# Moving a register load, the first rows' copies, four idle products and the order of the last products in a hybrid layer with a routed mixture of experts

## The chip, the cores and the metric

One core of one Trainium2 chip runs one launch. The metric is device microseconds of that launch; the time given is a median of runs without a profile. A profile is one more execution, taken by the hardware profiler. Times inside it count from the start of its span. Engines: PE multiplies (PEld loads its weights), DVE, ACT and POOL work on tiles in on-chip memory, SP issues most transfers.

## The reference

A pre-norm layer on 512 tokens of width 1024. The mixer and the router come first; what matters here is the mixture of experts behind them (one of 4 groups for each token, and two of its 8 experts):

```python
g_idx = jnp.argmax(g_logits, axis=-1)
top_p, top_i = lax.top_k(e_probs, TOP_K)
combine = (g_onehot[:, :, None] * (g_weight[:, None] * e_w)[:, None, :]).astype(x.dtype)
for g in range(N_GROUPS):
    h = jax.nn.silu(jnp.einsum('nd,edf->nef', xt, w_gate[g])) * jnp.einsum('nd,edf->nef', xt, w_up[g])
    out = out + jnp.einsum('nef,efd->nd', h * combine[:, g, :, None], w_down[g])
```

Then the result is added to the residual `h`, and a last RMSNorm gives the output. Each of 32 experts has three matrices of 2 MB in float32, 201 MB in all, and all of them are read.

## The kernel before, in words

The kernel is one function, `layer_kernel`, whose order on each engine is as written (a manual schedule): attention and spatial gating with the input projection, the output projection with the router inside it, then the experts in 16 pairs, then a tail.

**Router's end.** `rows_mm` (L853) sums where each expert's rows lie into `sps`; 8 products at L934 sum the tokens of each expert into `pos_ps`. `rows` (L858, L860) makes `gi`, the indices by which `gather` (L939) fetches the rows of later pairs from the stored `xn_d`. The rows of pair 0 don't come by gather: `first_rows` (L758) has them in PSUM tiles `px0` (`pf` in the profile), and `with_gain` (L973 on ACT, four copies; L975 on DVE, one) copies them into `xs0`.

**Counts.** From `pos_ps` DVE makes `cnt`, `cov`, `cop`, `tot` and `okt`. An expert has 64 slots (`SLOTS`); rows over them go to an overflow path (`over_1`, `over_2`, `gate_up_over`, `down_over`) under conditionals, `if_over`, one for each pair (L1215, L1174), whose counts are loaded into registers when they are reached (L1156). If the overflow is over 32 rows, a general path behind the tail does the rest: its count is `n_over`, loaded at L1153 on PE, ACT, DVE and SP; the conditional that reads it stands behind the tail.

**Pairs.** `gu(a)` and `gu(b)` are the gate and up products of the two experts (L1011, 16 products of 512 columns each), `act` the gate (L1017 to L1023), `down` (L1041) the down products into `y_0` and `y_1` for the two halves of the width, `results` (L1061 on ACT, L1062 on DVE) splits them into `yh` and `yl`, and `combine` of the pair before adds them to the tokens' rows with one-hot products (`oh`, L1051; `add_rows`, L1069) and DVE's `into_h` (L1075). From p = 1 on the overflow's conditionals stand behind `gu(b)` and behind `down`.

**Weights.** `load_next` issues transfers from SP in a fixed order, each 128 x 2048 floats, into 19 slots; each waits for PE to have read the slot's last content, and for an earlier transfer on its own semaphore. The last slot is in pool `mo`, which takes the memory of the router's pool `rw`.

**Tail.** For the last pair: `down` for `y_0`, `results`, `places` (`oh`), `down` for `y_1`, `results`; then `unit` (L1069, L1270, L1075) adds pair and overflow into `h` for four chunks and half 0 (`cl_0`), `squares` (L1260) sums for the norm, `gained` (L1275) multiplies by the gain, then half 1 (`cl_1`), `scale_3` (L1264, L1265), `finish` (L1279 to L1281) and the output.

`busy` (L183 to L187) issues products of the identity that nobody reads; before, it is called once, at the start:

```python
    def busy(pool, tag, n):

        ps = pool.tile([P, 512], F32, tag=tag, name="idle")
        for _ in range(n):
            nc.tensor.matmul(ps[:, :P], identf, identf, start=True, stop=True)
```

Of the kernel before, what the change touches and what calls it, by code (L numbers as in the profile page):

```python
# [8 lines left out]
F32 = mybir.dt.float32  # L9
# [3 lines left out]
AF = mybir.ActivationFunctionType  # L13
OP = mybir.AluOpType
AX = mybir.AxisListType
ET = mybir.EngineType
# [3 lines left out]
P = 128  # L20
T = 512
NCH = 4
D = 1024
KD = 8
# [6 lines left out]
OVER = 32  # L31
# [40 lines left out]
def layer_kernel(ctx, tc, xr, xT, gT, w_inT, w_inR, sgg, wsT, bsp, sbg, sog, w_out, ffg, wr, br,  # L72
                 w_gate, w_up, w_down, fing, out, dbg=None):
    nc = tc.nc
# [107 lines left out]
# [5 lines that stand above are left out]
# [371 lines left out]
    keep = ctx.enter_context(tc.tile_pool(name="keep", bufs=1, side="right"))  # L558
# [18 lines left out]
    slots = []  # L577

    def half_slot(pool, tag="b"):
        return lambda name: pool.tile([P, 2048], F32, tag=tag, name=name)  # L580

    def load_next(n=1):
        for _ in range(min(n, len(order))):
            e, i, j = order.pop(0)
            slots.append(slots.pop(0))
            t_ = slots[-1](f"r{e}_{i}_{j}")
            if i == 3:
                W[e, i, j] = t_.rearrange("p (j c) -> p j c", j=4)
                dma(W[e, i, j], w_down[e].rearrange("p (j c) -> p j c", j=4)[:, :, j * 512:(j + 1) * 512])
                continue  # L590
            dma(t_, (w_gate, w_up, w_down)[i][e][:, j * 2048:(j + 1) * 2048])
            for m in range(2):
                W[e, i, 2 * j + m] = t_[:, m * 1024:(m + 1) * 1024]
# [19 lines left out]
    op_ = wp.enter_context(tc.tile_pool(name="op", bufs=3, space=PS))  # L613
# [70 lines left out]
    rws = ExitStack()  # L684
    rw = rws.enter_context(tc.tile_pool(name="rw", bufs=1, side="right"))
# [4 lines left out]
    ffk = keep.tile([P, KD], F32, name="ffk")  # L690
# [51 lines left out]
    px0 = []  # L742
# [94 lines left out]
    def onehot(oh, lab, val, n):  # L837
        nc.vector.tensor_tensor(oh[:, :, :n], lab[:, None, :n].to_broadcast([P, 8, n]),
                                val.rearrange("p w c -> p (w c)")[:, :, None].to_broadcast([P, 8, n]), op=OP.is_equal)
# [14 lines left out]
                                     stop=w == 1 and c == NCH - 1, skip_group_check=True)  # L854

    def rows(ps):
        tl = rw.tile([P, 16], F32, name="stl")
        nc.vector.tensor_scalar(tl, ps[:, 0], PAD, None, op0=OP.add)  # L858
        gi = keep.tile([P, 16], I32, name="gi")
        nc.vector.scalar_tensor_tensor(gi, ps[:, 1], 128.0, tl, op0=OP.mult, op1=OP.add)  # L860
        return gi
# [81 lines left out]
    gather(xg, GI[:, 1:2])  # L943
    load_next(1)

    cnt = keep.tile([P, 82], I32, name="cnt")
# [8 lines left out]
    nc.vector.scalar_tensor_tensor(tot, cop[:, :1], float(OVER), tot, op0=OP.mult, op1=OP.add)  # L957
    nc.vector.tensor_scalar(okt, tot, float(OVER), None, op0=OP.is_le)

    rws.close()  # L960

    mo = ctx.enter_context(tc.tile_pool(name="mo", bufs=1))
    slots[:0] = [half_slot(mo)]
    load_next(1)
    xgo = mo.tile([P, D], F32, name="xgo")
    nc.gpsimd.memset(xgo, 0.0)
    XS, GU, SG, HT, YS, YT, OHT = {}, {}, {}, {}, {}, {}, {}

    def with_gain(xs, px, n):

        if n == 0:
            for k in range(4):
                nc.scalar.activation(xs[:, k], px[:, k, :xs.shape[2]], AF.Copy, scale=ffk[:, k:k + 1])  # L973
        else:
            nc.vector.tensor_tensor(xs[:, 4:], px[:, :, :xs.shape[2]],  # L975
                                    ffk[:, 4:, None].to_broadcast([P, 4, xs.shape[2]]), op=OP.mult)

    XS[0] = mo.tile([P, KD, P], F32, tag="xs", name="xs0")
    for n in range(2):
        with_gain(XS[0], px0[n], n)  # L980
    wp.close()
    attp.close()
    psg = ctx.enter_context(tc.tile_pool(name="psg", bufs=2, space=PS))
# [4 lines left out]
    def bank(name, *shape):  # L988
        return psm.tile([P, *shape], F32, tag="m", name=name)
# [23 lines left out]
    def gu(e):  # L1013
        GU[e] = psg.tile([P, F], F32, tag="gu", name=f"gu{e}")
        gate_up(e, GU[e], XS[e // 2][:, :, halves[e % 2][1]])
        SG[e] = mo.tile([P, 4, P], F32, tag="sg", bufs=2, name=f"sg{e}")
        nc.scalar.copy(SG[e], GU[e].rearrange("s (p j) -> s j p", j=4))  # L1017
# [14 lines left out]
    def down_weights(e, j, n):  # L1032
        return W[e, 3, n][:, j] if (e, 3, n) in W else W[e, 2, j][:, n * 512:(n + 1) * 512]

    def down(p, ns=(0, 1), js=range(4)):
        if p not in YS:
            YS[p] = [bank(f"y{p}_{n}", 512) for n in range(2)]
        for j, n in [(j, n) for j in js for n in ns]:
            for r, rs_ in halves:
                e = 2 * p + r  # L1040
                nc.tensor.matmul(YS[p][n][rs_], HT[e][:, j], down_weights(e, j, n),  # L1041
                                 start=j == 0, stop=j == 3, skip_group_check=True)
# [11 lines left out]
    def results(p, ns=(0, 1)):  # L1054

        if p not in YT:
            YT[p] = [mo.tile([P, D], F32R, tag=t_, name=f"{t_}{p}") for t_ in ("yh", "yl")]
        yh, yl = YT[p]
        for n in ns:
            cs = slice(n * 512, (n + 1) * 512)  # L1060
            nc.scalar.activation(yh[:, cs], YS[p][n], AF.Copy, scale=tab[:, 1, p:p + 1])  # L1061
            nc.vector.scalar_tensor_tensor(yl[:, cs], YS[p][n], tab[:, 1, p:p + 1], yh[:, cs].bitcast(F32),  # L1062
                                           op0=OP.mult, op1=OP.subtract)
# [45 lines left out]
    def over_1():  # L1109

        nc.vector.tensor_scalar(flat.rearrange("p (w c) -> p w c", w=2), pos, float(SLOTS), okt, op0=OP.is_ge, op1=OP.mult)
        for w in range(2):
            nc.scalar.copy(ovr[:, w, :, 2:], oab[:, w])
            nc.scalar.copy(ovr[:, w, :, 0], tokc)
            nc.scalar.copy(ovr[:, w, :, 1], cw[:, w])
        pr = bank("pr", 8)
        nc.tensor.matmul(pr, trib, flat, start=True, stop=False, skip_group_check=True)
        for j in range(1, 8):
            nc.tensor.matmul(pr[:, j:], onesb, flat[:, :8 - j], start=False, stop=j == 7, skip_group_check=True)
        rk = mo.tile([P, 2, NCH], F32, name="rk")  # L1120
        nc.vector.scalar_tensor_tensor(rk.rearrange("p w c -> p (w c)"), pr, 1.0, flat, op0=OP.add, op1=OP.mult)
        onehot(ohv, lab1, rk, P)
# [27 lines left out]

    EO = [ET.PE, ET.Activation, ET.DVE]
    over, so = {}, {}
    n_over = nc.values_load(cnt[:1, 32:33], engines=[*EO, ET.SP], min_val=0, max_val=2 * OVER * T)  # L1153

    def if_over(k):
        n = over[k] if k in over else nc.values_load(cnt[:1, k:k + 1], engines=EO, min_val=0, max_val=T)  # L1156
# [32 lines left out]
    for p in range(NP):  # L1189
        a, b = 2 * p, 2 * p + 1  # L1190
        last = p == NP - 1
        gu(a)
        if p == 0:
            over_1()
            pst = bank("pst", 2, NP)
            for i in range(8):
                for r, rs_ in halves:
                    nc.tensor.matmul(pst[rs_], ohf[:, i], cf[:, i, :, r::2], start=i == 0, stop=i == 7,
                                     skip_group_check=True)
            nc.vector.tensor_copy(tab[:, 1], pst[:, 1])  # L1200
            for c in range(NCH):
                nc.vector.tensor_scalar(tabt[:, c], pst[:, 0], PAD - c * P, None, op0=OP.add)
            load_next(4)
        if last:
            act(a)
            combine(p - 1, 0, 1, 2, 3, 4, 5)
        if p == 1:
            prep(xso, xgo, "o")
        gu(b)
        if p == 0:  # L1210
            over_2()
            clear(True)
            load_next(4)
        else:
            with if_over(66 + p):  # L1215
                gate_up_over(a)
                gate_up_over(b)
            load_next(8)
        if last:
            act(b)  # L1220
            combine(p - 1, 6, 7)
            down_over(p)
            break
        act(a)
        if p:
            combine(p - 1, 0, 1, 2, 3)
        act(b)
        if p:
            combine(p - 1, 4, 5, 6, 7)
        places(p)  # L1230
        prep_pair(p + 1)
        down(p)
        if p:
            down_over(p)
        load_next(4)
        results(p)
        if p == 2:
            oho = mo.tile([P, T], F32R, tag="cf", name="oho")
            for c in range(NCH):
                nc.vector.tensor_scalar(tabot[:, c:c + 1], tabo[:, :1], float(-c * P), None, op0=OP.add)  # L1240
            tokens(oho, tabot)
# [6 lines left out]
    p = NP - 1  # L1248
# [24 lines left out]
    def gained(c):  # L1273

        nc.vector.tensor_tensor(fin[c][:, :512], h[:, c, :512], finB[:, :512], op=OP.mult)  # L1275
# [7 lines left out]
    down(p, (0,))  # L1283
    results(p, (0,))
    places(p)
    down(p, (1,))
    results(p, (1,))
    for c in range(NCH):
        unit(c, 0)
        squares(c, 0)  # L1290
    for c in range(NCH):
        gained(c)
    for c in range(NCH):
        unit(c, 1)
# [158 lines left out]
```

## Time and profile before

| | |
|---|---|
| median of 3 runs | 750.23 us (748.41, 750.23, 751.82) |
| the profiled execution | 752.7 us, of which the span is 750.9 us |
| PE busy | 702.9 us, 94% of the span |
| DVE, ACT, POOL busy | 306.4, 226.3, 80.6 us |
| moved by DMA | 230.75 MB, mean 307 GB/s |
| expert phase | from 263.4 us (expert 0) to 723.5 us (the last `down`) |
| mean granted TensorE clock | 0.974 |

A busy PE says little here by itself: it is busy in nearly every stretch. What orders the expert phase is read from where PE waits, from how far apart the pairs start, and from what SP waits for between transfers. The time of the profiled execution is 2.5 us over the median; sums made in its times are carried over to the median.

### The profile page before, as it was taken

The numbers are of one execution on the slowest core, as the hardware profiler recorded it, in microseconds if no ns is written. First come the engines' busy times: TensorE is split into PE (matmuls) and PEld (weight loads), VectorE is DVE, ScalarE is ACT, GpSimd is POOL, SyncE is SP. The second block draws the span as 40 slices with busy tenths as digits, with TensorE's granted clock in tenths as the row PEclk, the third lists the DMA queues.
The fourth block names the chain that finished last, engine by engine and source line by source line (L and its number), as shares of the span: only waits on it lengthen the run. The fifth ranks groups of instructions, "written<-read, shape, count | busy, mean of one in ns | idle before, by whom it ended". The sixth has DMA issues, their size and how long they took to land. (4 is left out here: it accounts for less than half of the span.)

```text
span 750.9 us, 9252 instructions
## 1 busy us (share of the span) xinstructions
PE 702.9 (94%) x3454; PEld 398.3 (53%) x3454; DVE 306.4 (41%) x556; ACT 226.3 (30%) x383; POOL 80.6 (11%) x77
## 2 busy tenths in 40 slices
PE   8998999999999899999999999999999999898992
PEld 6776757678788746444453443434444444344431
DVE  5547748365675722323422403123133133042335
ACT  6564756655344412111211211111111111121114
POOL 0322212115121001000000000000000000000001
PEclk9989979899999999999999999999999999999996
DMA  8802010207539779699999999999999999999953
GB/s 277 339 8 105 2 56 29 84 1 266 225 129 397 279 314 412 266 419 419 419 420 418 418 422 419 420 419 418 420 418 416 421 417 419 419 418 421 404 205 117
DMA packets 42103, 230.75 MB, mean 307 GB/s; under 512 B 6136, under 2 KB 7800, under 8 KB 17968
## 3 DMA queue, kind: packets, MB, share of 16 engines
q1 hardware_dynamic: 39248, 223.81, 73.9%
q0 software_dynamic: 2208, 3.90, 1.4%
q10 hardware_dynamic: 576, 2.10, 0.7%
q8 instruction: 44, 0.72, 0.4%
q14 instruction: 27, 0.22, 0.1%
HBM read 229.69 MB, written 4.19 MB: 311 GB/s over the span
## 5 line engine op out<-in xcount | busy, mean ns | idle before, releaser
L1011 PE MATMUL gu<-r,xs 128*64 128x512 f32 x1024 | 230.8, 598 | 13.8 <-DMA r<-w_up 6.6
L1011 PEld LDWEIGHTS gu<-r,xs 128*64 128x64 f32 x1024 | 86.2, 137 | 154.8 <-issue 133.6
L1041 PE MATMUL y<-r,hg 128*64 128x512 f32 x512 | 114.2, 596 | 0.0
L1023 DVE TENSOR_TENSOR hg<-ft,gg 128x256 f32<-128x256 f32 x32 | 13.4, 419 | 228.7 <-ACT gg L1021 221.5
L1017 ACT COPY sg<-gu 128x512 f32<-128x512 f32 x32 | 18.8, 586 | 228.7 <-PE gu L1011 228.7
L1075 DVE TENSOR_TENSOR h<-cb,h 128x512 f32<-128x512 f32 x120 | 74.2, 679 | 0.0
L1041 PEld LDWEIGHTS y<-r,hg 128*64 128x64 f32 x512 | 36.0, 136 | 66.8 <-issue 51.6
L939 POOL DMA_INDIRECT xg<-xn_d,gi x15 | 15.5, 1036 | 376.9 <-PE px L997 365.9
L1062 DVE SCALAR_TENSOR_TENSOR yl<-y,tab,yh 128x512 fp32r<-128x512 f32 x32 | 23.8, 750 | 69.6 <-ACT yh L1061 68.2
L1069 PE MATMUL cb<-yh,oh 128*128 128x512 f32 x120 | 49.9, 415 | 0.0
L1069 PE MATMUL cb<-yl,oh 128*128 128x512 f32 x120 | 47.3, 394 | 0.0
L1061 ACT ACTIVATE yh<-y,tab 128x512 fp32r<-128x512 f32 x32 | 21.8, 687 | 78.6 <-PE y L1041 77.7
L115 PE MATMUL pT<-xhi,hl_w 128*128 128x512 f32 x80 | 34.3, 429 | 0.0
L117 PE MATMUL pT<-xhi,hl_w 128*128 128x512 f32 x80 | 33.0, 413 | 0.0
L116 PE MATMUL pT<-xlo,hl_w 128*128 128x512 f32 x80 | 32.9, 412 | 0.0
L110 POOL TENSOR_TENSOR hl_w<-wqk,hl_w 128x1024 fp32r<-128x1024 f32 x10 | 24.4, 2436 | 66.5 <-ACT hl_w L109 64.2
L115 PE MATMUL pR<-hl_w,xhi 128*128 128x512 f32 x64 | 26.1, 408 | 0.0
L1029 PEld LDWEIGHTS ft<-identf,sg 128*128 128x128 f32 x128 | 14.7, 140 | 21.3 <-issue 16.1
L116 PE MATMUL pR<-hl_w,xhi 128*128 128x512 f32 x64 | 25.6, 400 | 0.0
L117 PE MATMUL pR<-hl_w,xlo 128*128 128x512 f32 x64 | 25.4, 397 | 0.0
L973 ACT ACTIVATE xs<-px,ffk 128x128 f32<-128x128 f32 x60 | 17.2, 370 | 26.8 <-PE px L997 26.8
L1069 PEld LDWEIGHTS cb<-yh,oh 128*128 128x128 f32 x120 | 22.6, 188 | 4.4 <-DVE h L1075 0.2
(274 smaller groups left out, 939.9 us busy)
## 6 DMA issues: line engine op xcount, KB each, us to landing
r<-w_gate SPq DMA_DIRECT2D x64, 1024.0 KB, 20.0
r<-w_up SPq DMA_DIRECT2D x64, 1024.0 KB, 19.9
r<-w_down SPq DMA_DIRECT2D x64, 1024.0 KB, 20.1
wqk<-w_inT SPq DMA_DIRECT2D x10, 512.0 KB, 4.8
wr<-w_inR SPq DMA_DIRECT2D x8, 512.0 KB, 7.9
wo<-w_out SPq DMA_DIRECT2D x8, 512.0 KB, 4.7
xt<-xT SPq DMA_DIRECT2D x8, 256.0 KB, 5.0
h<-xr SPq DMA_DIRECT2D x4, 512.0 KB, 10.0
```

Source lines behind the costliest of these rows:

```text
L110: (nc.gpsimd if pool else nc.vector).tensor_tensor(lo, src, hi.bitcast(F32), op=OP.subtract)
L115: nc.tensor.matmul(ps, lh, rh, start=first, stop=False)
L116: nc.tensor.matmul(ps, lh, rl, start=False, stop=False)
L117: nc.tensor.matmul(ps, ll, rh, start=False, stop=last)
L973: nc.scalar.activation(xs[:, k], px[:, k, :xs.shape[2]], AF.Copy, scale=ffk[:, k:k + 1])
L1011: nc.tensor.matmul(ps[rs_], xs[:, k], w, start=k == 0, stop=k == KD - 1, skip_group_check=True)
L1017: nc.scalar.copy(SG[e], GU[e].rearrange("s (p j) -> s j p", j=4))
L1041: nc.tensor.matmul(YS[p][n][rs_], HT[e][:, j], down_weights(e, j, n), start=j == 0, stop=j == 3, skip_group_check=True)
L1061: nc.scalar.activation(yh[:, cs], YS[p][n], AF.Copy, scale=tab[:, 1, p:p + 1])
L1062: nc.vector.scalar_tensor_tensor(yl[:, cs], YS[p][n], tab[:, 1, p:p + 1], yh[:, cs].bitcast(F32), op0=OP.mult, op1=OP.subtract)
L1069: nc.tensor.matmul(ps, OHT[p][:, c * P:(c + 1) * P], y[:, n * 512:(n + 1) * 512], start=first and i == 0, stop=last and i == 1, skip_group ...
L1075: nc.vector.tensor_tensor(h[:, c, cs], ps, h[:, c, cs], op=OP.add)
```

## The change

It does four things.

1. The load of `n_over` into registers (L1153 before) moves into the loop over pairs, to p = 2 behind `results`.
2. The copies of the first rows (`with_gain` into `xs0`) and the opening of pool `mo` with its slot come ahead of the counts. For that `stl` is taken from pool `keep` and no longer from `rw`, and `xgo` (the overflow's rows) is cleared on DVE inside `over_1`, no longer on POOL at this place.
3. `busy(op_, "o", 4)`: four products of the identity on PE, behind the router's last products.
4. In the tail `y_1` is made in two halves of its four steps, around the four units of half 0; `results` for `y_1` comes behind two of the four `gained`.

```diff
     def rows(ps):
-        tl = rw.tile([P, 16], F32, name="stl")
+        tl = keep.tile([P, 16], F32, name="stl")
...
     gather(xg, GI[:, 1:2])
     load_next(1)
 
+    rws.close()
+
+    mo = ctx.enter_context(tc.tile_pool(name="mo", bufs=1))
+    slots[:0] = [half_slot(mo)]
+    load_next(1)
...
+    XS[0] = mo.tile([P, KD, P], F32, tag="xs", name="xs0")
+    for n in range(2):
+        with_gain(XS[0], px0[n], n)
+    busy(op_, "o", 4)
+
...
     cnt = keep.tile([P, 82], I32, name="cnt")
...
-    rws.close()
...
-    nc.gpsimd.memset(xgo, 0.0)
...
-    XS[0] = mo.tile([P, KD, P], F32, tag="xs", name="xs0")
-    for n in range(2):
-        with_gain(XS[0], px0[n], n)
...
+        nc.vector.memset(xgo, 0.0)
         pr = bank("pr", 8)
...
-    n_over = nc.values_load(cnt[:1, 32:33], engines=[*EO, ET.SP], min_val=0, max_val=2 * OVER * T)
...
         if p == 2:
+            n_over = nc.values_load(cnt[:1, 32:33], engines=[*EO, ET.SP], min_val=0, max_val=2 * OVER * T)
...
-    down(p, (1,))
-    results(p, (1,))
+    down(p, (1,), (0, 1))
     for c in range(NCH):
         unit(c, 0)
         squares(c, 0)
-    for c in range(NCH):
+    down(p, (1,), (2, 3))
+    for c in range(2):
+        gained(c)
+    results(p, (1,))
+    for c in range(2, NCH):
         gained(c)
```

PE between the router's last products (`pos_ps`) and expert 0 (`gu`), before:

```order
L934 LDWEIGHTS onesb
L934 MATMUL pos_ps<-oab,onesb 128x32
L1153 TENSOR_LOAD cnt
L1011 MATMUL gu_2194<-r_0_0_1207,xs_2131 64x512
L1011 MATMUL gu_2194<-r_1_0_1209,xs_2131 64x512
```

and after the change:

```order
L934 LDWEIGHTS onesb
L934 MATMUL pos_ps<-oab,onesb 128x32
L186 MATMUL idle<-identf 128x128 x4
L1012 MATMUL gu_2185<-r_0_0_1207,xs_2119 64x512
L1012 MATMUL gu_2185<-r_1_0_1209,xs_2119 64x512
```

The load of the count is gone from this place, and four idle products stand there; the load now stands behind pair 2, ahead of the seventh expert.

DVE at the same place, as a difference (`pf` is the PSUM tile of the first rows):

```order
 L858 TENSOR_SCALAR stl<-sps 128x16
 L860 SCALAR_TENSOR_TENSOR gi<-sps,stl 128x16
-L953 CAST cnt<-pos_ps 128x32
-L954 TENSOR_SCALAR cov<-pos_ps 128x32
+L960 TENSOR_TENSOR xs_2119<-pf_1958,ffk 128x512
+L975 CAST cnt<-pos_ps 128x32
+L976 TENSOR_SCALAR cov<-pos_ps 128x32
 L723 TENSOR_REDUCE tot<-cov 128x1
 L723 TENSOR_REDUCE cop<-cov 128x16
-L957 SCALAR_TENSOR_TENSOR tot<-cop,tot 128x1
-L958 TENSOR_SCALAR okt<-tot 128x1
-L975 TENSOR_TENSOR xs_2131<-pf_1958,ffk 128x512
```

DVE's half of the copies moves from behind the counts to directly behind `gi`.

DVE in the tail, before:

```order
L1051 TENSOR_TENSOR oh_6734<-slotf,tabt 128x512
L1062 SCALAR_TENSOR_TENSOR yl_6731<-y_1_6721,tab,yh_6730 128x512
L1075 TENSOR_TENSOR h<-cl_0_6746,h 128x512
L1075 TENSOR_TENSOR h<-cl_0_6752,h 128x512
L1075 TENSOR_TENSOR h<-cl_0_6758,h 128x512
L1075 TENSOR_TENSOR h<-cl_0_6764,h 128x512
L1275 TENSOR_TENSOR fin_6706<-h,fin_6708 128x512 x2
L1275 TENSOR_TENSOR fin_6707<-h,fin_6708 128x512 x2
L1075 TENSOR_TENSOR h<-cl_1_6774,h 128x512
```

and after the change:

```order
L1052 TENSOR_TENSOR oh_6739<-slotf,tabt 128x512
L1076 TENSOR_TENSOR h<-cl_0_6745,h 128x512
L1076 TENSOR_TENSOR h<-cl_0_6751,h 128x512
L1076 TENSOR_TENSOR h<-cl_0_6757,h 128x512
L1076 TENSOR_TENSOR h<-cl_0_6763,h 128x512
L1277 TENSOR_TENSOR fin_6711<-h,fin_6713 128x512 x2
L1063 SCALAR_TENSOR_TENSOR yl_6736<-y_1_6726,tab,yh_6735 128x512
L1277 TENSOR_TENSOR fin_6712<-h,fin_6713 128x512 x2
L1076 TENSOR_TENSOR h<-cl_1_6779,h 128x512
```

`yl` for the second half moves from ahead of the four adds to behind them and behind two of the gains.

## Rows read from the trace of the kernel before

**Rows 1.** Stretch: us; busy of PE, PEld, DVE, ACT, POOL; clock, DMA, GB/s.

```profile
300.00:310.00 10.00, 9.60 (x49) 4.35 (x47) 1.83 (x5) 1.30 (x4) 0.00 (x0) 1.00 0.37 126
...
400.00:450.00 50.00, 47.97 (x245) 20.78 (x241) 10.60 (x18) 7.97 (x16) 0.99 (x1) 1.00 1.01 419
```

**Rows 2.** Who waited for whom, PE, 262 to 740: us, times, longest.

```profile
PE gu L1011 <- DMA r<-w_up: 6.6, 6, 1.3
```

**Rows 3.** Timeline of PE: start, length, line, operation [idle before <- releaser].

```profile
527.50 13.95 PE L1011 MATMUL gu<-r,xs 128*64 128x512 f32 x64 [0.31 <-PEq L1174]
...
554.75 13.95 PE L1011 MATMUL gu<-r,xs 128*64 128x512 f32 x64 [0.31 <-PEq L1174]
...
640.59 7.91 PE L1011 MATMUL gu<-r,xs 128*64 128x512 f32 x34 [0.31 <-PEq L1174]
...
671.22 7.91 PE L1011 MATMUL gu<-r,xs 128*64 128x512 f32 x34 [0.31 <-PEq L1174]
```

**Rows 4.** Timeline of SP's issues of weights.

```profile
268.77 0.33 SPq L591 DMA_DIRECT2D r<-w_up  x1
...
292.04 0.33 SPq L591 DMA_DIRECT2D r<-w_gate  x1
307.05 0.33 SPq L591 DMA_DIRECT2D r<-w_up  x1
...
351.85 0.33 SPq L591 DMA_DIRECT2D r<-w_gate  x1
361.63 0.33 SPq L591 DMA_DIRECT2D r<-w_up  x1
```

**Rows 5.** Timeline of all engines around the start of expert 0.

```profile
257.99 2.05 PE L758 MATMUL pf<-own,h 128*128 128x128 f32 x16 [0.89 <-DVE own L750]
...
260.46 0.17 DVE L860 SCALAR_TENSOR_TENSOR gi<-sps,stl 128x16 int32<-128x16 f32 x1
...
260.79 1.14 ACT L973 ACTIVATE xs<-pf,ffk 128x128 f32<-128x128 f32 x4 [1.90 <-DVE gi L860]
...
261.58 0.69 DVE L975 TENSOR_TENSOR xs<-pf,ffk 128x512 f32<-128x512 f32 x1
262.19 0.14 DVE L1133 CAST cnt<-tot 128x1 int32<-128x1 f32 x1
...
263.42 8.78 PE L1011 MATMUL gu<-r,xs 128*64 128x512 f32 x32 [2.92 <-issue]
...
265.96 0.22 DVE L1111 TENSOR_SCALAR fl<-pos,okt 128x8 bf16<-128x8 f32 x1
...
272.14 0.18 PE L1117 MATMUL pr<-fl,trib 128*128 128x8 bf16 x1
```

**Rows 6.** Instructions of line 1153 on PE's sequencer: length ns, start.

```profile
L1153 PEldq TENSOR_LOAD <-cnt x1: 492/492/492, 262.5 to 262.5; - x1
```

**Rows 7.** Stretch of the first half of expert 0, columns as in rows 1.

```profile
264.00:267.50 3.50, 3.50 (x12) 1.26 (x10) 2.08 (x9) 0.00 (x0) 0.19 (x1) 0.51 0.52 208
```

**Rows 8.** Timeline of the tail.

```profile
728.60 0.68 DVE L1051 TENSOR_TENSOR oh<-slotf,tabt 128x512 fp32r<-128x512 f32 x1
...
730.52 0.50 PE L1069 MATMUL cl<-yh,oh 128*128 128x512 f32 x1
...
730.64 0.69 ACT L1061 ACTIVATE yh<-y,tab 128x512 fp32r<-128x512 f32 x1 [2.75 <-PE y L1041]
...
731.37 0.75 DVE L1062 SCALAR_TENSOR_TENSOR yl<-y,tab,yh 128x512 fp32r<-128x512 f32 x1 [2.08 <-ACT yh L1061]
...
732.03 2.47 DVE L1075 TENSOR_TENSOR h<-cl,h 128x512 f32<-128x512 f32 x4
...
734.42 2.48 DVE L1275 TENSOR_TENSOR fin<-h,fin 128x512 f32<-128x512 f32 x4
...
735.93 0.39 PE L1270 MATMUL cl<-yo2b,oho 128*128 128x512 f32 x1
736.83 1.28 DVE L1075 TENSOR_TENSOR h<-cl,h 128x512 f32<-128x512 f32 x2
```

More of the change, by code (lines that the diff above doesn't have):

```diff
@@ L944, in layer_kernel, with with_gain @@
     load_next(1)
+    rws.close()
+    mo = ctx.enter_context(tc.tile_pool(name="mo", bufs=1))
+    slots[:0] = [half_slot(mo)]
+    load_next(1)
+    xgo = mo.tile([P, D], F32, name="xgo")
+    XS, GU, SG, HT, YS, YT, OHT = {}, {}, {}, {}, {}, {}, {}
+    def with_gain(xs, px, n):
+        if n == 0:
+            for k in range(4):
+                nc.scalar.activation(xs[:, k], px[:, k, :xs.shape[2]], AF.Copy, scale=ffk[:, k:k + 1])
+        else:
+            nc.vector.tensor_tensor(xs[:, 4:], px[:, :, :xs.shape[2]],
+                                    ffk[:, 4:, None].to_broadcast([P, 4, xs.shape[2]]), op=OP.mult)
+    XS[0] = mo.tile([P, KD, P], F32, tag="xs", name="xs0")
+    for n in range(2):
+        with_gain(XS[0], px0[n], n)
+    busy(op_, "o", 4)
     cnt = keep.tile([P, 82], I32, name="cnt")
@@ L958, in layer_kernel @@
     nc.vector.tensor_scalar(okt, tot, float(OVER), None, op0=OP.is_le)
-    rws.close()
[L962 to L965, printed above, removed]
-    nc.gpsimd.memset(xgo, 0.0)
[L967 to L976, printed above, removed]
-    XS[0] = mo.tile([P, KD, P], F32, tag="xs", name="xs0")
-    for n in range(2):
-        with_gain(XS[0], px0[n], n)
     wp.close()
```

## Prediction, made before the change was run

> **What bounds the kernel now.** I read the expert phase first, from the table of busy time by stretch, and looked at the last two columns. From 310 us to the last pairs the weights stream at 419 GB/s, a DMA share of 1.01 (the stretch 400 to 450 stands for the rest); the one hole in it is in the stretch 300 to 310, at 126 GB/s [rows 1]. A transfer is 128 x 2048 floats, 1.05 MB, so 2.50 us at that rate, and a pair of experts needs 12 of them, 30.0 us. Then the list of who waited for whom: in the phase PE waits for weights six times, 6.6 us in all [rows 2]. PE's timeline shows where: pairs start 27.25 us apart in the middle (527.50, 554.75) and 30.63 us apart late (640.59, 671.22) [rows 3]. So PE eats a store of loaded weights early, and late it runs at the pace of the stream. The end is set by the last moment at which the stream started up again, plus the bytes left. The queue's own timeline gives that moment: SP issues at 292.04, then nothing until 307.05, because the slots it needs are given back by PE behind the first conditional of the pair p = 1; before that its restart at 268.77 waits for PE to read the first half of expert 0's weights [rows 4]. Both moments hang on PE's progress from expert 0 on. What PE gains or loses in starting expert 0 therefore moves the stream and the end, one to one; what it loses behind 307, while it still leads the stream, does not.
>
> Expert 0 starts late. Its first product runs at 263.42, after 2.92 us of idleness (so from 260.50, where the router's last product ends) put down to PE's own issue [rows 5]. What it does there is the load of the general path's count: the count is ready when the cast of `tot` ends on DVE (262.19 + 0.14 = 262.33), PE's load of it takes 0.49 us, from 262.5 [rows 6], and about 0.4 us later the first product runs. Expert 0 then takes 8.72 us to the next operation (263.42 to 272.14) [rows 5], where a full-speed pair of experts takes 13.95 us, 6.98 each [rows 3]. The clock tells why: between 264.0 and 267.5 its mean is 0.51, the lower of its two levels, 1.2 GHz [rows 7].
>
> **The change part by part.**
>
> *The count's load moves to the third pair.* PE no longer waits for it. What ends last for expert 0 then? Its first product needs `gi` (260.46 + 0.17 = 260.63) and the first copy of `xs`; with the copies where they are, ACT's first of four ends about 261.1 (260.79 and a quarter of 1.14) [rows 5]. So alone this would start expert 0 near 261.2, 2.2 us earlier.
>
> *The copies of the first rows move ahead of the counts.* `stl` now lies in another pool, so ACT's copies wait for the last router product that reads that memory, not for `gi`; they can start by 260.3 to 260.79. DVE's half comes straight after `gi`, about 260.75 to 261.45, where it ran 261.58 to 262.27 [rows 5]. The ninth of expert 0's 16 products is the first that needs it, 3.5 us after the start, half of 6.98. With the idle products below, both copies are there in time either way: this part is worth 0 to 0.5 us alone, 0 here.
>
> *Four idle products.* They stand on PE behind the router's last product. The row of the last first-row products gives their price: 16 records in 2.05 us, two to a product (first_rows has eight products a chunk) [rows 5], so four take 1.02 us, from 260.50 to 261.5. At half clock they would take 2.05 us and end at 262.55; below 1.0 I see no reason to go. I take 261.5, the row's own rate. They cost up to 0.7 us of start (0.3 against the unmoved copies), and fill the idleness that stands ahead of the fall of the clock. If the clock then holds, expert 0 takes 6.98 us and not 8.72, 1.74 us less.
>
> Start 263.42 - 261.5 = 1.9 us, clock 1.7 us, together **3.6 us** at the end of expert 0 (268.5 for 272.14). What is late next there? The small products behind expert 0 need `fl`; in the trace it ends at 266.18 (265.96 + 0.22) [rows 5], with a load ahead of it that is gone now. The cleared `xgo`, moved from POOL to DVE, stands behind `fl`: at most twice DVE's 0.69 us for a half-sized copy [rows 5], 1.4 us, over by 267.6. Nobody needs it before 268.5, so 0.
>
> *The load in the third pair.* On PE, ACT, DVE and SP it stands behind pair 2, near 347 us (three pairs of some 28 us behind 263.42). On PE it costs 0.5 us (its row) to 1.1 us (262.33 to 263.42, all that lies between count and product); the cover is PE's lead over the stream, 3.4 us a pair (30.63 - 27.25), used up only after 582 (554.75 + 27.25), where pairs still started at PE's own pace [rows 3]. Without that cover it would cost the 1.1. On SP I take the same 0.5, and behind it wait the weights: from 307.05 to 351.85 SP issues 24 transfers, 60 us of work at 2.50, so the stream has work until about 367, while SP itself stands until 361.63 [rows 4]. The slack is about 5 us, and the wait in front is for work of the first 300 us: 0.
>
> *The tail.* PE now does half of `y_1`, the four `cl_0` units, the other half, then `cl_1`. In the trace `oh` is ready at 729.28, the first unit runs at 730.52, and DVE is the engine without a gap from 731.37: `yl` 0.66 us, four adds into `h` 2.39, four gains 2.41, and the `cl_1` adds start at 736.83 [rows 8]. New: the units start at 729.35, the adds near 730.3, paced by PE at 0.7 each (24 products from 730.52 to 735.93 are 0.235 apart, three to a unit), and end near 733.05; two gains to 734.25; then `yl` must wait, since PE's second half of `y_1` comes behind the units (732.25 to 734.2) and ACT's copy `yh` takes 0.7 more, 734.9; `yl` to 735.6, two gains to 736.8. The `cl_1` adds start at 736.8 again: DVE starts 1.0 us earlier and stands 0.9 us more. I take 0, with -0.4 to +0.5 as the errors of these six steps.
>
> Sum against the profiled execution (span 750.9, 752.7 with what lies around it): 752.7 - 3.6 = 749.1. The runs without a profile have a median of 750.23, 2.5 lower; the same gain gives 750.2 - 3.6 = **746.6 us**, 0.48% less. About 0.5% (3.75 us) is what a measurement of this kernel can tell from no change; the forecast lies just at that line.
>
> **The rivals.**
> *A. Only the start is gained.* Either the clock falls in spite of the idle products, or it doesn't fall here in the timed runs, so that there is nothing to save. For it: one profile shows one fall, and the timed runs differ by 3.4 us among themselves. Gain 1.9: 748.3 us. The Trainium skill (TensorE: Matmul & The Clock Gate, section "What's actually happening") says that what watches the engine isn't in step with the kernel's start, so that the place of a change differs from run to run. By that rule some timed runs of before have no fall here; no row can show it.
> *B. Off the path.* PE starts earlier but the stream's end doesn't move: something else than PE's slots holds SP at 268 or 307. Against it: both waits are put down to PE's instructions and its conditional. Gain 0: 750.2 us.
> *C. Slower, by the clock in the tail.* PE now has two pauses there: 0.5 us before `cl_0` and up to 1.5 us before `cl_1` (734.2 to 735.6). If the clock falls at them, the second half of `y_1` and twelve products of 0.235 us, or the last twelve, double: 1.7 + 2.8 = 4.5 us at most. It decides the sign from 3.6 us on, with the gain of the start, and from 1.9 us on with A. Price at most: 750.2 - 3.6 + 4.5 = 751.1 us, 752.8 with A. Against it: in the trace the clock held through six waits for weights of up to 1.3 us [rows 2].
>
> **How the numbers follow.** Forecast 0.58, A 0.27, B 0.10, C 0.05. The forecast's own spread: the start 261.2 to 262.5, the tail -0.4 to +0.5, some 0.7 us for a median of three: 745.3 to 748.0. The range reaches to A and its spread and leaves B and C out: **745.3 to 749.0**. Below 746.48 lies somewhat under half of the forecast (0.27), some more for a fall that is spared elsewhere (0.05): faster 0.32. Slower by over 3.75 us: only the far end of C, 0.03. The rest, 0.65, is the same.
>
> **What would show it.** In the changed kernel's timeline: four idle products from 260.5 to 261.5, expert 0 at 261.5, the next operation 7.0 us later, clock 1.0 from 260 to 268; SP's restart 3.5 us earlier than 268.77 and its other restart near 303.5; late pairs still 30.6 us apart, with PE still waiting for weights; a 0.5 to 1.1 us pause of PE near 344 with no hole in the 419 GB/s; `cl_1` adds as far behind the start of `y_0` as now. I am wrong if the restarts move and the end doesn't, if the late pairs change their pace, or if the first product waits for something that I don't see, such as the gather on POOL.

## The result, and the profile after

The changed kernel takes **746.21 us** (median of 8 runs, 743.66 to 749.37) against 750.19 (8 runs beside it, 748.41 to 753.86): ratio 0.9938, 95% interval 0.9911 to 0.9965. A second comparison, further down, gave 0.9972 (0.9943 to 1.0001). The forecast was 746.6 us, range 745.3 to 749.0, a ratio of 0.9952, which lies between the two.

The profiled execution is 744.16 us with a span of 742.3, and 750.9 - 742.3 = 8.6 us is well over twice the forecast gain of 3.6. Half of it is not the change. The first DVE operation behind the router, `stl`, starts at 260.25 before and at 255.87 after, 4.38 us earlier, and nothing ahead of it was edited: the granted clock in 90 to 120 us is 0.83 before and 1.00 after, in 135 to 150 us 0.77 and 0.89. How many such falls an execution has differs from run to run, and that is most of the scatter of the times: over the 100 runs of the kernel before that stood beside the experiments, time and mean clock go together with a correlation of -0.91. So from here on every place in a trace is told **behind the start of `stl`** of the same trace. That start before, from DVE's timeline:

```profile
260.25 0.17 DVE L858 TENSOR_SCALAR stl<-sps 128x16 f32<-128x16 f32 x1 [1.65 <-PE sps L853]
```

From there the span has 490.7 us left before and 486.4 after: 4.2 us.

The start of expert 0 after, timeline of all engines (start, length, engine, line, operation, [idle before <- releaser]):

```profile
255.87 0.17 DVE L858 TENSOR_SCALAR stl<-sps 128x16 f32<-128x16 f32 x1 [1.65 <-PE sps L853]
255.92 1.15 ACT L958 ACTIVATE xs<-pf,ffk 128x128 f32<-128x128 f32 x4 [1.40 <-PE sps L853]
255.98 1.14 PE L186 MATMUL idle<-identf 128*128 128x128 f32 x8
256.08 0.17 DVE L860 SCALAR_TENSOR_TENSOR gi<-sps,stl 128x16 int32<-128x16 f32 x1
256.29 0.69 DVE L960 TENSOR_TENSOR xs<-pf,ffk 128x512 f32<-128x512 f32 x1
257.04 7.09 PE L1012 MATMUL gu<-r,xs 128*64 128x512 f32 x32
...
260.36 0.22 DVE L1112 TENSOR_SCALAR fl<-pos,okt 128x8 bf16<-128x8 f32 x1
260.74 0.91 DVE L1117 MEMSET xgo<- 128x1024 f32 x1 [0.15 <-PE gu L1012]
264.06 0.18 PE L1119 MATMUL pr<-fl,trib 128*128 128x8 bf16 x1
```

Against [rows 5]: the first product came 263.42 - 260.25 = 3.17 us behind `stl` and now comes 257.04 - 255.87 = 1.17 us behind it, 2.00 us sooner. It follows the idle products with no idle time of its own. From there to the next operation, `pr`, it was 8.72 us and is 264.06 - 257.04 = 7.02. ACT's copies start ahead of `gi`, with the wait put down to `sps`, as the new place of `stl` allows. The cleared `xgo` ends at 261.65, well ahead of 264.06.

Stretches after (columns as in [rows 1]; the clock is the third number from the end):

```profile
256.00:260.00 4.00, 4.00 (x28) 1.98 (x25) 3.70 (x21) 1.07 (x4) 1.77 (x3) 1.00 0.73 251
260.00:264.00 4.00, 4.00 (x20) 1.15 (x16) 1.50 (x3) 0.00 (x0) 0.00 (x0) 1.00 0.81 267
339.00:347.00 8.00, 7.28 (x36) 2.99 (x36) 2.44 (x7) 0.73 (x2) 0.00 (x0) 1.00 1.01 418
400.00:450.00 50.00, 48.27 (x252) 22.39 (x250) 14.97 (x26) 8.14 (x19) 1.98 (x2) 1.00 1.01 419
```

No fall at expert 0, where [rows 7] had 0.51. SP's issues of weights after, the places of [rows 4]:

```profile
260.72 0.33 SPq L591 DMA_DIRECT2D r<-w_up  x1
...
283.97 0.33 SPq L591 DMA_DIRECT2D r<-w_gate  x1
298.98 0.33 SPq L591 DMA_DIRECT2D r<-w_up  x1
...
343.97 0.33 SPq L591 DMA_DIRECT2D r<-w_gate  x1
353.91 0.33 SPq L591 DMA_DIRECT2D r<-w_up  x1
```

Both restarts moved by what expert 0 gained: 8.52 behind `stl` became 4.85 (3.67 sooner), 46.80 became 43.11 (3.69). The load of the count in the third pair, instructions of its line (length ns, start), and PE's next product:

```profile
L1239 PEldq TENSOR_LOAD <-cnt x1: 313/313/313, 339.5 to 339.5; - x1
...
L1239 SPq TENSOR_LOAD <-cnt x1: 468/468/468, 344.4 to 344.4; - x1
```

```profile
339.83 1.51 PE L1012 MATMUL gu<-r,xs 128*64 128x512 f32 x6 [0.72 <-PEq L1239]
```

PE stands 0.72 us where a pair's start has 0.31, so it costs 0.4; SP loads between its issues of 343.97 and 353.91, and the stream around it holds 418 GB/s. The late pairs and the waits there, PE's timeline and then its list of waits (us, times, longest):

```profile
632.12 7.91 PE L1012 MATMUL gu<-r,xs 128*64 128x512 f32 x34 [0.31 <-PEq L1175]
...
663.09 7.91 PE L1012 MATMUL gu<-r,xs 128*64 128x512 f32 x34 [0.31 <-PEq L1175]
```

```profile
PE gu L1012 <- DMA r<-w_up: 5.3, 5, 1.3
```

They are 30.97 us apart, where 12 transfers take 30.0, and PE still waits for weights: the stream still sets the pace. The first product of `y_0` before, and then the tail after with its own `y_0`:

```profile
723.51 7.09 PE L1041 MATMUL y<-r,hg 128*64 128x512 f32 x32
```

```profile
715.08 5.37 PE L1042 MATMUL y<-r,hg 128*64 128x512 f32 x24
...
721.00 0.47 PE L1070 MATMUL cl<-yh,oh 128*128 128x512 f32 x1 [0.55 <-DVE oh L1052]
...
721.98 2.76 DVE L1076 TENSOR_TENSOR h<-cl,h 128x512 f32<-128x512 f32 x4 [1.12 <-PE cl L1272]
...
723.94 1.94 PE L1042 MATMUL y<-r,hg 128*64 128x512 f32 x8
724.65 1.28 DVE L1277 TENSOR_TENSOR fin<-h,fin 128x512 f32<-128x512 f32 x2
725.92 0.69 ACT L1062 ACTIVATE yh<-y,tab 128x512 fp32r<-128x512 f32 x1 [0.16 <-PE y L1042]
726.65 0.75 DVE L1063 SCALAR_TENSOR_TENSOR yl<-y,tab,yh 128x512 fp32r<-128x512 f32 x1 [0.71 <-ACT yh L1062]
...
728.51 1.28 DVE L1076 TENSOR_TENSOR h<-cl,h 128x512 f32<-128x512 f32 x2
```

`y_0` starts at 715.08, so the adds of `cl_1` into `h` start 13.43 us behind it; before it was 736.83 - 723.51 = 13.32 [rows 8]. DVE starts its adds 1.6 us earlier against `y_0` and gives it back, 0.71 us of it waiting for `yh`.

The 4.23 us in pieces: start of expert 0 2.00, expert 0 itself 1.70, from there to SP's second restart 0, from that restart to `y_0` 0.36 (416.46 became 416.10), from `y_0` to DVE's last operation 0.46 (20.32 became 19.86), from there to the end -0.28. Two of these pieces can't be put down to the change: the stretch from the restart to `y_0` takes 415.97 to 416.79 us over the 14 traces of the next section, and the 7.09 us from DVE's last operation to the end are the shortest of all in this trace of the kernel before, where the other 13 have 7.34 to 7.56. The change's own part is 3.70 us at expert 0 and 0.46 at the end.

### The profile page after: what moved, and what is told of

Same layout as the page of the kernel before. It is cut to its first block, busy times and chain, and to the rows that moved or that the text cites. A ratio compares the mean times of both kernels' runs of the same rounds, so it can differ in the third digit from the quotient of the medians.

```text
span 742.3 us, 9269 instructions
## 1 busy us (share of the span) xinstructions
PE 698.5 (94%) x3462; PEld 395.2 (53%) x3462; DVE 305.8 (41%) x557; ACT 226.3 (30%) x383; POOL 77.8 (10%) x76
## 5 line engine op out<-in xcount | busy, mean ns | idle before, releaser
L1012 PE MATMUL gu<-r,xs 128*64 128x512 f32 x1024 | 228.4, 595 | 10.0 <-DMA r<-w_up 5.3
L1018 ACT COPY sg<-gu 128x512 f32<-128x512 f32 x32 | 18.8, 587 | 225.2 <-PE gu L1012 225.2
L115 PE MATMUL pT<-xhi,hl_w 128*128 128x512 f32 x80 | 32.9, 412 | 0.0
L117 PE MATMUL pT<-xhi,hl_w 128*128 128x512 f32 x80 | 31.6, 395 | 0.0
```

The source lines that it names most:

```text
L115: nc.tensor.matmul(ps, lh, rh, start=first, stop=False)
L117: nc.tensor.matmul(ps, ll, rh, start=False, stop=last)
L1012: nc.tensor.matmul(ps[rs_], xs[:, k], w, start=k == 0, stop=k == KD - 1, skip_group_check=True)
```

## The experiments

My theory was the prediction's: the load alone held expert 0, the pause let the clock fall, and the stream hands on what PE gains there. The rivals: the idle products or the copies do it, the fall was chance, or the end hangs on something else. All traces in one table, in us: how far the first product of expert 0, SP's second restart and the first product of `y_0` lie behind `stl`; how long expert 0 takes to the next operation; how far the end of DVE's last operation lies behind `y_0`; what is left of the span behind `stl`; and the timed ratio to the kernel before, beside it.

| kernel | start | expert 0 | restart | y_0 | y_0 to last DVE | left of span | ratio (95%) |
|---|---|---|---|---|---|---|---|
| before | 3.17 | 8.72 | 46.80 | 463.26 | 20.32 | 490.7 | 1 |
| before, again | 3.18 | 8.55 | 46.64 | 463.11 | 20.33 | 491.0 | |
| clear only | 3.17 | 8.72 | 46.80 | 463.19 | 20.33 | 491.1 | |
| copies only | 3.12 | 8.72 | 46.75 | 463.03 | 19.74 | 490.1 | 0.9996 (0.9965-1.0027) |
| idle only | 3.15 | 7.02 | 45.08 | 461.05 | 20.33 | 488.8 | 0.9964 (0.9933-0.9995) |
| load back | 3.12 | 7.02 | 45.05 | 461.05 | 19.86 | 488.3 | 0.9957 (0.9927-0.9987) |
| load only | 1.01 | 7.02 | 42.94 | 458.92 | 20.33 | 486.7 | 0.9949 (0.9917-0.9981) |
| 16 idle | 3.85 | 7.02 | 45.78 | 461.82 | 19.87 | 489.0 | 0.9986 (0.9955-1.0018) |
| delay in the middle | 1.17 | 7.02 | 43.10 | 459.49 | 19.87 | 486.7 | 0.9940 (0.9909-0.9971) |
| no idle | 0.59 | 7.02 | 42.52 | 458.61 | 19.85 | 485.8 | 0.9928 (0.9896-0.9959) |
| old tail | 1.17 | 7.02 | 43.10 | 459.48 | 19.74 | 486.6 | 0.9899 (0.9869-0.9928) |
| no idle, old tail | 0.59 | 7.02 | 42.51 | 459.30 | 19.75 | 486.4 | 0.9933 (0.9902-0.9965) |
| after | 1.17 | 7.02 | 43.11 | 459.21 | 19.86 | 486.4 | 0.9938 (0.9911-0.9965) |
| after, again | 1.17 | 7.03 | 43.10 | 459.36 | 19.85 | 486.5 | 0.9972 (0.9943-1.0001) |

An interval is some 4.5 us wide, so the traces decide and the ratios only have to agree.

**Load only.** In the kernel before, one line goes and comes back in the third pair:

```diff
-    n_over = nc.values_load(cnt[:1, 32:33], engines=[*EO, ET.SP], ...)
...
         if p == 2:
+            n_over = nc.values_load(cnt[:1, 32:33], engines=[*EO, ET.SP], ...)
```

> The kernel before with one edit: PE's, ACT's, DVE's and SP's load of the general path's count moves to the third pair. Nothing else is moved, no idle products, the old tail. My theory: the load alone held expert 0, so its first product comes about 0.7 us behind the router's last product instead of 2.92 us, 2.2 us sooner; and the pause is then too short for the clock to fall, so expert 0 takes 7.0 us instead of 8.72. Together 3.9 us: 746.3 us, as the whole change. Rival 1, the idle products are what holds the clock: the start is 2.2 us sooner, expert 0 still takes 8.7 us, 748.0 us. Rival 2, the copies of the first rows must move too: ACT's copies stay behind the counts, the start is gained by less than 1.5 us, 748.7 us or more.

It took 746.49 us beside 752.63 for the kernel before. The timeline of PE:

```profile
257.79 7.09 PE L1011 MATMUL gu<-r,xs 128*64 128x512 f32 x32 [0.75 <-issue]
```

The start comes 2.16 us sooner, the clock does not fall, and no idle products were needed for it. This one line brings 3.9 of the 4.2 us: 2.16 at the start and 1.70 in expert 0.

**Load back.** The changed kernel with that line at its old place.

> The changed kernel with the load of the general path's count back at its old place ahead of expert 0; copies moved ahead, idle products and new tail stay. My theory: the load is what held the start, so the first product of expert 0 comes 3.0 to 3.2 us behind the start of stl on DVE, as before (3.17), 2.0 us later than in the changed kernel (1.17). The idle products leave a pause of 1.9 us. If the clock holds then, expert 0 takes 7.0 us and the time is 748.2 us; if it falls as before, 8.7 us and 749.9 us. Rival, the copies and the idle products made the gain and the load can stand where it stood: the start stays near 1.2 us behind stl and the time near 746.2 us.

It took 749.04 us beside the same 752.63. PE's timeline:

```profile
259.81 7.09 PE L1012 MATMUL gu<-r,xs 128*64 128x512 f32 x32 [1.88 <-POOL fold L1144]
```

The start is back at 3.12, so the load sets it, and the clock holds over a pause of 1.88 us: the first of the two branches that were named.

**No idle products.** The changed kernel without `busy(op_, "o", 4)`.

> The changed kernel without the four idle products behind the router. My theory: the first product comes 0.3 to 0.7 us sooner than with them (in the changed kernel it comes 1.17 us behind the start of stl on DVE, here 0.5 to 0.9 us), the clock holds without them, expert 0 takes 7.0 us, and the time is 0.3 to 0.7 us under that of the changed kernel: 745.7 us. Rival, the idle products hold the clock: expert 0 takes 8.7 us at a clock near 0.5, and the time is 1.0 to 1.4 us over that of the changed kernel: 747.4 us.

The median is 746.28 us beside 752.63. The timeline of PE:

```profile
259.28 7.09 PE L1011 MATMUL gu<-r,xs 128*64 128x512 f32 x32 [0.34 <-ACT xs L958]
```

The start comes 0.58 us sooner, now behind ACT's first copy, and expert 0 still takes 7.02 us. With the load gone the idle products hold no clock; they cost 0.58 us. Against load only, whose copies stand behind the counts, this start is 0.42 us sooner (0.59 for 1.01). So the copies ahead are worth something once the load is gone, and the four idle products take it back: the whole change starts expert 0 at 1.17 us, 0.16 later than the one line alone.

**The kernel before, again.**

> The kernel before, unchanged, for a second profile. My theory: the pause of 2.9 us ahead of expert 0 is what brings the fall of the clock, so it is there again: expert 0 takes 8.7 us at a clock near 0.5 in its first half. Rival, the fall stood there by chance in the one profile: expert 0 takes 7.0 us at clock 1.0, and the pause costs no clock.

The one run took 749.26 us. PE's timeline, and the stretches around expert 0:

```profile
259.70 8.62 PE L1011 MATMUL gu<-r,xs 128*64 128x512 f32 x32 [2.93 <-issue]
```

```profile
259.00:260.00 1.00, 0.30 (x2) 0.32 (x4) 1.00 (x3) 0.00 (x0) 0.99 (x3) 0.71 0.98 393
260.00:263.00 3.00, 3.00 (x9) 0.81 (x7) 2.33 (x12) 0.00 (x0) 0.46 (x3) 0.53 0.68 276
263.00:264.00 1.00, 1.00 (x8) 0.45 (x6) 0.00 (x0) 0.00 (x0) 0.00 (x0) 1.00 0.00 0
```

The fall is there again, here from some 0.3 us ahead of the first product (a mean of 0.71 in the first stretch).

**Idle products only.** The kernel before with nine idle products in the pause, ahead of the load:

```diff
     for n in range(2):
         with_gain(XS[0], px0[n], n)
+    busy(op_, "o", 9)
     wp.close()
```

> The kernel before with nine idle products (2.3 us) behind the router's last product, ahead of PE's load of the count; nothing else. They fill most of the pause of 2.92 us and should not move the start of expert 0, 3.17 us behind the start of stl on DVE. My theory, the pause brings the fall of the clock and filling it holds the clock: expert 0 takes 7.0 us instead of 8.72 us, the time is 1.7 us under that of the kernel before. Rival, the fall is there by chance and not in most runs: same time as before within 0.5 us.

It took 749.45 us beside 752.36. PE's timeline, and the stretch of expert 0:

```profile
258.79 2.25 PE L186 MATMUL idle<-identf 128*128 128x128 f32 x18
...
261.83 7.09 PE L1012 MATMUL gu<-r,xs 128*64 128x512 f32 x32 [0.79 <-PE idle L186]
```

```profile
261.80:268.80 7.00, 6.97 (x32) 2.64 (x32) 2.69 (x12) 0.00 (x0) 0.82 (x3) 1.00 0.64 241
```

The start stays (3.15), the clock is 1.00, expert 0 takes 1.70 us less and SP's second restart is 1.72 us sooner. That is the clock's term by itself. At expert 0 all four traces with a pause of 2.87 us or more have the fall, the ten with 1.88 us or less have none, and here filling the pause took the fall away: the pause brings it.

The length of a pause alone does not tell a fall, though. In five of the 14 traces (after, load only, idle only, 16 idle, old tail) the clock also falls once near 456 to 460 us, just behind two pauses of 1.12 and 0.74 us that the other nine traces have as well. The stretch behind these two pauses in after, and then in after again:

```profile
456.00:460.00 4.00, 4.00 (x20) 0.88 (x19) 1.41 (x2) 0.67 (x2) 0.00 (x0) 0.57 1.01 420
```

```profile
459.50:463.50 4.00, 4.00 (x26) 1.15 (x28) 1.41 (x2) 0.75 (x2) 0.00 (x0) 1.00 1.01 422
```

What decides there stays open.

**Sixteen idle products** in the place of four, in the changed kernel.

> The changed kernel with 16 idle products ahead of expert 0 instead of four: twelve more at 0.255 us each, PE starts expert 0 3.1 us later and loses nothing else. My theory: what PE loses there moves SP's restarts and the end one to one, so SP's two restarts behind expert 0 come 3.1 us later against the start of stl (in the changed kernel 4.85 and 43.1 us behind it) and the time is 749.3 us. Rival B of the prediction, off the path: the restarts may move, the end doesn't, 746.2 us.

The median is 750.41 us beside 752.36. PE's first product of expert 0, and SP's second restart:

```profile
261.44 7.09 PE L1012 MATMUL gu<-r,xs 128*64 128x512 f32 x32
```

```profile
303.37 0.33 SPq L591 DMA_DIRECT2D r<-w_up  x1
```

The twelve took 0.22 us each, not 0.255, so PE starts 2.68 us later. The restart comes 2.67 later, `y_0` 2.61, the end 2.6: one to one. Rival B, off the path, is out.

**The same delay in the middle.** The changed kernel with 16 idle products at the end of the sixth pair:

```diff
         results(p)
+        if p == 5:
+            busy(psm, "m", 16)
         if p == 2:
```

> The changed kernel with 16 idle products on PE at the end of the pair p = 5 (4.1 us of PE's time in the middle of the stream). My theory: PE leads the stream there and the loss is made good by fewer waits for weights late, so the time stays at 746.2 us within 0.7, and the weights keep 419 GB/s. Rival, PE is the bound in the middle or its slots hold the stream: 750.3 us, or a hole in the stream of a microsecond or more behind the idle products.

It took 747.15 us beside 752.36. PE's timeline, and the stretch around it:

```profile
395.59 13.95 PE L1012 MATMUL gu<-r,xs 128*64 128x512 f32 x64 [0.31 <-PEq L1175]
422.84 3.81 PE L186 MATMUL idle<-identf 128*128 128x128 f32 x32 [0.31 <-PEq L1175]
426.57 13.95 PE L1012 MATMUL gu<-r,xs 128*64 128x512 f32 x64
```

```profile
422.00:430.00 8.00, 7.69 (x52) 4.85 (x50) 1.50 (x2) 1.09 (x2) 0.00 (x0) 1.00 1.02 421
```

The pairs are 30.98 us apart instead of 27.25, 3.7 us lost, the stream goes on at 421 GB/s, and what is left of the span grows by 0.25 us, no more than the traces of one kernel differ by (0.3 us between the two of before). PE's waits for `w_up` shrink from 5.3 to 4.2 us. What PE loses while it leads the stream is nearly free, as the prediction said of the load in the third pair. The fall near 456 us in after is a second case of it: the pair there takes 37.47 us from start to start where after again has 36.13, and what is left of the span is the same (486.4 and 486.5).

**The old tail** in the changed kernel.

> The changed kernel with the tail in its order of before. My theory: the new order is worth nothing, so the time is that of the changed kernel, 746.2 us, within 0.5 us, and the adds of cl_1 into h start 13.3 us behind the first product of y_0, where the changed kernel has 13.4 and the kernel before 13.3. Rival 1, the new order gains a microsecond or more outside what the one trace shows: 747.2 us or more. Rival 2, it costs that much through PE's two pauses: 745.2 us or less.

It took 744.75 us beside 752.63. The adds of `cl_1` start 730.06 - 716.74 = 13.32 us behind `y_0`: the tail is worth 0.1 us in the trace, on the wrong side. The ratio, 0.9899, is the lowest of all and would fit rival 2; but the two kernels without idle products, which differ in the tail alone, have 0.9928 (new) and 0.9933 (old), on two chips. Whether the old tail is better by more than 0.1 us in the timed runs stays open.

**No idle products and the old tail.**

> The changed kernel without the idle products and with the tail of before: what is left is the load in the third pair, the copies ahead of the counts and the clear on DVE. From the traces so far the idle products cost 0.58 us of start and the new tail 0.1 us, and the clock held without them. My theory: expert 0 starts 0.6 us behind the start of stl instead of 1.17 us, takes 7.0 us, and the span behind stl is 0.6 us shorter than the changed kernel's 486.4 us: 485.8 us, the time some 0.6 us under that of the changed kernel run beside it. Rival: the idle products are needed for the clock in some of the runs, then the time is 0 to 1 us over it.

It took 745.36 us beside 750.09. Expert 0 starts at 0.59 as expected, but what is left of the span is 486.4 and not 485.8 us: the stretch from SP's second restart to `y_0` took 416.8 us where the other traces of this table have 416.0 to 416.5. The ratio is the better of the two that ran side by side, with a mean over the runs of 746.09 against 748.62; the mean granted clock of those runs was also the higher, 0.981 against 0.978. So 0.6 us can't be told apart here, and this version is as good as the changed kernel or a little better.

**The changed kernel, again.**

> The changed kernel unchanged, beside the kernel without idle products. My theory: the ratio to before stays near 0.994, 486.4 us from the start of stl to the end, expert 0 at clock 1.0. Rival: the first comparison was favoured by falls of the clock ahead of the change, then the ratio is 0.996 to 0.998.

It took 748.75 us beside 750.09. The ratio is what the rival expected, the trace what I expected: 1.17, 7.03, 486.5. Both hold: what the change gives behind the router is the same each time, while the timed runs differ by what happens ahead of it. The second comparison went against the change: its runs had a mean clock of 0.978 beside 0.979 for the kernel before, though they spare a fall. Whether the first was favoured is not shown, as there are no clocks for its runs of the kernel before.

**Clear only and copies only.** The 0.5 us at the very end was not foreseen. It shows in every kernel with the copies ahead and the clear on DVE, whichever tail, load or idle products it has. In the kernel before, alone: the clear on DVE; then, without it, the copies and the opening of `mo` with its slot ahead of the counts, with `stl` in pool `keep`.

> The kernel before with one edit: the clear of xgo runs on DVE behind fl and no longer on POOL. In the traces of kernels with the clear on DVE and the copies ahead, the last product on DVE ends 19.8 us behind the first product of y_0; in the others 20.3 us. Theory 1, the clear on POOL does it: 19.8 us here. Theory 2, it is the order of the copies: 20.3 us here. Either way expert 0 starts 3.2 us behind stl, as in the kernel before.

> The kernel before with one edit: stl in the kept pool and the copies of the first rows ahead of the counts. Load of the count, clear on POOL and tail as before, no idle products. Theory: the load holds the start, so expert 0 still comes 3.2 us behind stl and takes 8.7 us at half clock in its first half. At the end, by elimination, the moved copies are what takes 0.5 us off the last products: the last one on DVE ends 19.8 us behind the first product of y_0 and the time is 0.5 us under that of before. Rival 1: the end stays at 20.3 us and the 0.5 us needs the clear and the copies together. Rival 2: the copies gain at the start too, expert 0 comes less than 3.0 us behind stl.

Clear only took 753.68 us in its one run and keeps 20.33, so it is not the clear. Copies only took 751.31 us beside 751.72 and has 19.74: it comes with the move of the copies. Expert 0 starts at 3.12 with a fall, so while the load stands there they gain nothing at the start. The end in the second trace of the kernel before, and in that of copies only:

```profile
736.75 3.60 SPq L1281 DMA_DIRECT2D res<-fin  x4
...
737.14 0.63 ACT L1260 ACTIVATE sq<-h 128x512 f32<-128x512 f32 x1 [0.41 <-DVE ms L1264]
...
739.21 0.75 DVE L1280 SCALAR_TENSOR_TENSOR fin<-h,rs,fin 128x512 f32<-128x512 f32 x1 [0.44 <-POOL rs L1265]
```

```profile
739.49 3.11 SPq L1282 DMA_DIRECT2D res<-fin  x4
...
739.57 0.63 ACT L1261 ACTIVATE sq<-h 128x512 f32<-128x512 f32 x1
...
740.71 1.41 DVE L1281 SCALAR_TENSOR_TENSOR fin<-h,rs,fin 128x512 f32<-128x512 f32 x2 [0.16 <-POOL rs L1266]
```

Between SP's first issue of results and ACT's last square lie 0.39 us in the one and 0.08 in the other; the last scaling on DVE hangs on it by way of POOL. Both programs let that square wait for the same add into `h`. The traces show where the 0.3 us lies: ACT's sequencer ends its wait for that add 0.35 us before the square in all five traces without the move, and 0.04 us before it in all nine with it. They also show one difference in ACT's own stream of instructions: the nine have one wait more on it (a semaphore instruction at L1018, at 262.1 us in copies only, ahead of the first `sg`), so that all that follows stands one place later. Whether that shift moves the 0.3 us, no run tests; the cause stays open.

## Why the prediction was right

*The bound.* Right. The restarts moved by 3.67 and 3.69 us (3.5 was forecast), 2.68 us of delay at expert 0 came out at the end as 2.6, 3.7 us in the middle as 0.25.

*The load.* Right: 2.16 us alone, 2.2 forecast. In the third pair it cost PE 0.4 us, below the lower of the two bounds (0.5 and 1.1): the load took 313 ns there, not the row's 492. It was hidden on PE and on SP.

*The start with idle products.* 1.9 forecast, 2.00 measured; they cost 0.58 us of start, 0.3 to 0.7 forecast.

*The clock.* 1.74 forecast, 1.70 measured. But the step that the idle products "fill the idleness that stands ahead of the fall of the clock" put it down to the wrong part in this kernel: load only and no idle products hold the clock as well. Taking the load away shortens the pause, and that is enough; the idle products only do it where the load stays.

*Copies ahead.* 0 at the start beside the idle products: right, and without them 0.42 us, within the 0 to 0.5 that were given for it. The 0.46 us in the last operations of the kernel was missed, and its cause is not settled.

*Tail.* 0 forecast, +0.11 measured, by the steps named: DVE stood 0.71 us for `yh`, 0.9 forecast.

*The sum.* 3.6 forecast; 4.1 to 4.5 us in the two traces each of before and after, of which 3.5 to 3.7 are the two forecast terms and 0.5 the end's, the missed term. The two timed comparisons give 0.62% and 0.28%, 4.7 and 2.1 us, and 3.6 lies between. That the first median came within 0.4 us of the forecast is luck in part: the second median of the same kernel is 2.5 us higher.

*Rivals.* A (no clock gained): the fall stood in all four traces with the long pause, so there was something to save. The timed runs have no stretches to read; the ratio of idle only, 0.9964 (0.9933 to 0.9995), lies below 1 and has the 1.7 us (0.9977) in its interval. The Trainium skill (TensorE: Matmul & The Clock Gate, section "What's actually happening") has the place of a change differ from run to run. The traces agree: the fall begins from 0.3 us ahead of the first product to 0.9 us behind it. It moved, but most of it lay in expert 0 each time. B is out by the sixteen idle products. C: the clock stays 1.00 through both pauses of the tail (0.55 and 0.79 us in after), in all six traces with the new order. The falls near 456 us show that pauses of about that size can be followed by one, so C was no idle fear.

## What to carry to other kernels

Read what a wait at a stage's start costs from the queue that the stage feeds: here a microsecond of PE ahead of the first expert was a microsecond at the end, and the same microsecond five pairs later was free. A register load belongs where its engine has a lead, not where it opens a pipeline; and with the pause gone, the work that was put there to hold the clock was only a cost here. Where a kernel's time scatters by more than the change is worth, lay the traces on a common event just ahead of the change and compare from there.

## What the hardware showed that I had not expected

The granted clock falls at places ahead of the change that differ between executions of the same code: over all traces `stl` started between 255.87 and 260.82 us, a range of 5 us. The 100 timed runs of the kernel before that stood beside the experiments go from 745.41 to 756.97 us, with mean granted clocks of 0.987 and 0.970 at these ends.

Two pauses of 1.12 and 0.74 us in the middle of the expert phase were followed by a fall in five of 14 traces, and one pause of 1.88 us ahead of expert 0 by none in the one trace that has it. The fall in the middle cost nothing at the end.

A load of a register from `cnt` took 492 ns on PE where it came 0.2 us behind the write, and 313 ns on PE, 278 on ACT and 304 on DVE in the third pair, 80 us behind it. How long the write is past does not explain it: at the old place DVE's load took 556 ns though it came 2.4 us behind the write, and on SP it took 482 ns there and 468 in the third pair.

Moving ACT's copies at 256 us changed when ACT's last square starts 480 us later by 0.3 us, with the same waits of that square in the program and one wait more far ahead of it.
